# RMS norm on one core: ScalarE squares without summing, GpSimd scales part of the rows, VectorE code is aligned, the last tile is loaded whole

## The chip, the cores and the metric

The kernel runs on one core of one Trainium2 chip. The metric is device time in microseconds (us), the median of several executions. The *span* of a profile is a little shorter than that time: 160.0 against 161.79 us in the profiled execution of the kernel before. All runs told here are with a granted clock of 1.00.

In the profile's lines, DVE is VectorE, ACT is ScalarE, POOL is GpSimd, SP is SyncE (it issues all large transfers here), PE is TensorE, and DMA stands for the core's sixteen transfer engines. SBUF is the on-chip memory that holds the tiles; PSUM is a second one, which takes the squares and, after the change, gamma. "L95" is line 95 of the kernel whose profile is shown; an edit can shift the numbers by a few lines.

## The reference

```python
x: (16, 1024, 512) float32;  gamma: (512,) float32, all ones
rms = np.sqrt(np.mean(x ** 2, axis=-1, keepdims=True) + 1e-5)
return (x / rms * gamma).astype(np.float32)
```

There are 16,384 rows of 512 elements: 33.55 MB to read and as much to write.

## The kernel before

The rows make four tiles; a tile is 128 partitions of 32 rows each (8 MB). The kernel keeps three tiles in SBUF at once, so tile 3 goes into the slot of tile 0 and can be loaded only when tile 0 has been stored (its load is issued at 81.86 us, after a wait of 8.6 us for that store). SyncE issues everything in one fixed order:

```python
groups = [(t, g) for t in range(4) for g in range(0, R, G)]     # R = 32, G = 8 rows
slot_of = [0, 1, 2, 0]
def transfers(t, g):                 # after the group at row g of tile t has been scaled
    if (t, g) == (0, 0):
        store(0, 0, 0, 1);  load(1, 1, 0, 32);  load(2, 2, 0, 16)
        store(0, 0, 1, 2);  load(2, 2, 16, 32)
    elif (t, g) == (0, 24):  store(0, 0, 2, 32)
    elif (t, g) == (1, 8):
        store(1, 1, 0, 16)
        load(3, 0, 0, 16)            # tile 3 in two halves
        load(3, 0, 16, 32)
    elif (t, g) == (1, 24):  store(1, 1, 16, 32)
    elif (t, g) == (2, 24):  store(2, 2, 0, 32)
    elif (t, g) == (3, 8):   store(3, 0, 0, 16)
    elif (t, g) == (3, 24):  store(3, 0, 16, 32)
```

Half of the groups are squared and summed by ScalarE alone, row by row; for the other half ScalarE squares four rows at a time into PSUM and VectorE sums them. VectorE scales every row:

```python
if (g // G) % 2:
    for h in range(0, G, H):                                     # H = 4
        sq = psum.tile([P, H, D], fp32, name="sq")
        nc.scalar.activation(out=sq, in_=slots[slot][:, g+h : g+h+H, :], func=AF.Square)
        nc.vector.tensor_reduce(out=ss[:, h : h+H], in_=sq, axis=..., op=OP.add)
else:
    for r in range(G):
        nc.scalar.activation(out=sq_scratch, in_=slots[slot][:, g+r, :],
                             func=AF.Square, accum_out=ss[:, r : r+1])
... sqrt on ScalarE, reciprocal on VectorE ...
for r in range(G):
    nc.vector.scalar_tensor_tensor(out=row, in0=row, scalar=rstd[:, r : r+1],
                                   in1=gamma_b, op0=OP.mult, op1=OP.mult)   # gamma_b in SBUF
```

Of the kernel before, what the change touches and what calls it, by code (L numbers as in the profile page):

```python
# [1 line left out]

# [4 lines left out]


@with_exitstack
def kernel(  # L10
    ctx: ExitStack,
    tc: tile.TileContext,
    x: bass.AP,
    gamma: bass.AP,
    out: bass.AP,
):
    nc = tc.nc
    P = nc.NUM_PARTITIONS
    eps = 1e-5
    fp32 = mybir.dt.float32  # L20
    AF = mybir.ActivationFunctionType
    OP = mybir.AluOpType

    xf = x.flatten_outer_dims()
    of = out.flatten_outer_dims()
    N, D = xf.shape
    R = 32
    G = 8
    H = 4
    assert N == 4 * P * R  # L30

    xv = xf.rearrange("(t p r) d -> t p r d", p=P, r=R)
    ov = of.rearrange("(t p r) d -> t p r d", p=P, r=R)

    const = ctx.enter_context(tc.tile_pool(name="const", bufs=1))
    stats = ctx.enter_context(tc.tile_pool(name="stats", bufs=4))
    psum = ctx.enter_context(tc.tile_pool(name="psum", bufs=2, space=bass.MemoryType.PSUM))

    slots = [const.tile([P, R, D], fp32, name=f"slot{i}") for i in range(3)]

    def load(t, slot, r0, r1):
        nc.sync.dma_start(out=slots[slot][:, r0:r1], in_=xv[t][:, r0:r1])  # L42

    def store(t, slot, r0, r1):
        nc.sync.dma_start(out=ov[t][:, r0:r1], in_=slots[slot][:, r0:r1])

    load(0, 0, 0, 8)
    load(0, 0, 8, 32)

    gamma_row = const.tile([1, D], fp32)  # L50
    nc.scalar.dma_start(out=gamma_row, in_=gamma.unsqueeze(0))
    ones_col = const.tile([1, P], fp32)
    nc.vector.memset(ones_col, 1.0)  # L53
    gamma_psum = psum.tile([P, H, D], fp32, name="sq")
    nc.tensor.matmul(gamma_psum[:, 0], ones_col, gamma_row, start=True, stop=True)  # L55
    gamma_b = const.tile([P, D], fp32)
    nc.vector.tensor_copy(out=gamma_b, in_=gamma_psum[:, 0])  # L57

    eps_t = const.tile([P, 1], fp32)
    nc.vector.memset(eps_t, eps)  # L60
    sq_scratch = const.tile([P, D], fp32)

    def row_stats(slot, g):
        ss = stats.tile([P, G], fp32, name="ss")
        rms = stats.tile([P, G], fp32, name="rms")
        rstd = stats.tile([P, G], fp32, name="rstd")
        if (g // G) % 2:
            for h in range(0, G, H):
                sq = psum.tile([P, H, D], fp32, name="sq")
                nc.scalar.activation(out=sq, in_=slots[slot][:, g + h : g + h + H, :], func=AF.Square)  # L70
                nc.vector.tensor_reduce(  # L71
                    out=ss[:, h : h + H], in_=sq, axis=mybir.AxisListType.X, op=OP.add
                )
        else:
            for r in range(G):
                nc.scalar.activation(  # L76
                    out=sq_scratch,
                    in_=slots[slot][:, g + r, :],
                    func=AF.Square,
                    accum_out=ss[:, r : r + 1],  # L80
                )
        nc.scalar.activation(out=rms, in_=ss, func=AF.Sqrt, bias=eps_t, scale=1.0 / D)  # L82
        nc.vector.reciprocal(out=rstd, in_=rms)  # L83
        return rstd

    def apply(slot, g, rstd):
        for r in range(G):
            nc.vector.scalar_tensor_tensor(  # L88
                out=slots[slot][:, g + r, :],
                in0=slots[slot][:, g + r, :],  # L90
                scalar=rstd[:, r : r + 1],
                in1=gamma_b,
                op0=OP.mult,
                op1=OP.mult,
            )  # L95

    groups = [(t, g) for t in range(4) for g in range(0, R, G)]
    slot_of = [0, 1, 2, 0]

    def transfers(t, g):  # L100
        if (t, g) == (0, 0):
            store(0, 0, 0, 1)
            load(1, 1, 0, 32)
            load(2, 2, 0, 16)
            store(0, 0, 1, 2)
            load(2, 2, 16, 32)
        elif (t, g) == (0, 24):
            store(0, 0, 2, 32)
        elif (t, g) == (1, 8):
            store(1, 1, 0, 16)  # L110
            load(3, 0, 0, 16)
            load(3, 0, 16, 32)
        elif (t, g) == (1, 24):
            store(1, 1, 16, 32)
        elif (t, g) == (2, 24):
            store(2, 2, 0, 32)
        elif (t, g) == (3, 8):
            store(3, 0, 0, 16)
        elif (t, g) == (3, 24):
            store(3, 0, 16, 32)  # L120

    ahead = row_stats(0, 0)
    for k, (t, g) in enumerate(groups):
        rstd = ahead
        if k + 1 < len(groups):
            tn, gn = groups[k + 1]
            ahead = row_stats(slot_of[tn], gn)
        apply(slot_of[t], g, rstd)
        transfers(t, g)


# [1 line left out]
_INS = ['x', 'gamma']  # L133
_OUTS = [((16, 1024, 512), 'float32')]


# [23 lines left out]
```

## Time and profile before

| | before |
|---|---|
| time, median | 162.27 us (3 runs), 162.15 us in the rounds with the change |
| transfer queue, share of sixteen engines' span | 97.9% |
| VectorE busy | 122.6 us (77%) |
| ScalarE busy | 80.1 us (50%) |
| GpSimd busy | 0.2 us |
| last store issued | 146.62 us |

The page of the kernel before: the span in 40 slices (each digit is the busy share of a slice in tenths; the DMA row is the mean of the sixteen transfer engines), and the queue that carries all of x.

```profile
span 160.0 us, 409 instructions
...
DVE  0101928999999509999999999999999999996000
...
DMA  5999999699699999997999999999996996999993
...
q1 hardware_dynamic: 2160, 67.11, 97.9%
```

The costliest groups of instructions of the page (line, engine, operation, output and inputs, shape, count; busy time and mean ns of one; idle time just before them and what ended it).

```profile
L88 DVE SCALAR_TENSOR_TENSOR slot<-slot,rstd,gamma_b 128x512 f32<-128x512 f32 x128 | 85.8, 741 | 0.1
L76 ACT ACTIVATE sq_scratch<-slot 128x512 f32<-128x512 f32 x64 | 40.0, 625 | 10.0 <-DMA slot<-in_x_dram 8.7
L70 ACT ACTIVATE sq<-slot 128x2048 f32<-128x2048 f32 x16 | 29.8, 1865 | 18.8 <-DVE ss L71 11.5
L71 DVE TENSOR_REDUCE ss<-sq 128x4 f32<-128x2048 f32 x16 | 35.9, 2277 | 3.6 <-ACT sq L70 3.6
```

The transfers bound this kernel. From the records of single packets, no gap shows in any of the sixteen engines between the first load and the last store; the dips of the digits are the edges of packets of up to 2.6 us. Compute matters only where a store is issued too late to keep the queue full. The timeline of VectorE and SyncE at the end (start, length in us, what) shows how near that is: the last store goes out at 146.62 us, right after VectorE's last row.

```profile
136.62 9.97 DVE L88 SCALAR_TENSOR_TENSOR slot<-slot,rstd,gamma_b 128x512 f32<-128x512 f32 x15
146.62 0.33 SPq L45 DMA_DIRECT2D out_dram<-slot  x1
```

### The profile page before, as it was taken

Reading aid. Unit: us, or ns where it says so; the run is one execution under the profiler, and the core shown is the slowest. Engines: PE = TensorE matmul, PEld = TensorE weight load, DVE = VectorE, ACT = ScalarE, POOL = GpSimd, SP = SyncE. Lnnn points to the kernel's source line nnn. Section 1 sums busy time; section 2 is a strip of 40 time slices with the busy share of each in tenths; the row PEclk is TensorE's granted clock in tenths of the full one; section 3 lists DMA queues with packets and bytes.
Section 4 is the critical chain, followed back from the end, with each engine's and each line's share of the span. In section 5 each row is a group of like instructions: output and inputs, shape, how many; then the busy total and the mean of one; then the engine's idle time right before and its main releaser. Section 6 shows DMA issues by size and latency. Waiting matters only on the chain.

```text
span 160.0 us, 409 instructions
## 1 busy us (share of the span) xinstructions
PE 2.0 (1%) x2; PEld 0.5 (0%) x2; DVE 122.6 (77%) x163; ACT 80.1 (50%) x162; POOL 0.2 (0%) x4
## 2 busy tenths in 40 slices
PE   4000000000000000000000000000000000000000
PEld 1000000000000000000000000000000000000000
DVE  0101928999999509999999999999999999996000
ACT  3098029991291999996900960069709950000000
POOL 0000000000000000000000000000000000000000
DMA  5999999699699999997999999999996996999993
GB/s 197 524 393 393 430 487 508 279 524 491 295 395 396 456 467 434 494 461 323 445 393 475 426 410 426 475 410 410 491 524 295 508 491 295 467 434 410 426 475 147
DMA packets 2164, 67.13 MB, mean 420 GB/s; under 512 B 241, under 2 KB 241, under 8 KB 498
## 3 DMA queue, kind: packets, MB, share of 16 engines
q1 hardware_dynamic: 2160, 67.11, 97.9%
q14 instruction: 2, 0.02, 0.0%
q10 hardware_dynamic: 2, 0.00, 0.0%
HBM read 33.56 MB, written 33.55 MB: 419 GB/s over the span
## 4 chain that ended last, share of the span: by engine, by line
DVE 67%; DMA 14%; ACT 7%; issue 2%; DVEq 0%; SPq 0%
DVE slot L88 48%; DVE ss L71 18%; DMA slot<-in_x_dram 14%; ACT sq_scratch L76 3%; ACT sq L70 3%; DVE rstd L83 1%; ACT rms L82 1%; DVEq L155 0%; SPq L42 0%
## 5 line engine op out<-in xcount | busy, mean ns | idle before, releaser
L88 DVE SCALAR_TENSOR_TENSOR slot<-slot,rstd,gamma_b 128x512 f32<-128x512 f32 x128 | 85.8, 741 | 0.1
L76 ACT ACTIVATE sq_scratch<-slot 128x512 f32<-128x512 f32 x64 | 40.0, 625 | 10.0 <-DMA slot<-in_x_dram 8.7
L70 ACT ACTIVATE sq<-slot 128x2048 f32<-128x2048 f32 x16 | 29.8, 1865 | 18.8 <-DVE ss L71 11.5
L71 DVE TENSOR_REDUCE ss<-sq 128x4 f32<-128x2048 f32 x16 | 35.9, 2277 | 3.6 <-ACT sq L70 3.6
L82 ACT ACTIVATE rms<-ss,eps_t 128x8 f32<-128x8 f32 x16 | 4.6, 297 | 26.2 <-DVE ss L71 26.0
L83 DVE RECIPROCAL rstd<-rms 128x8 f32<-128x8 f32 x16 | 3.1, 196 | 16.3 <-ACT rms L82 16.3
L76 ACT ACTIVATION_READ_ACCUMULATOR sq_scratch<-slot 128x1 f32 x64 | 11.9, 186 | 0.0
L57 DVE COPY gamma_b<-sq 128x512 f32<-128x512 f32 x1 | 0.7, 691 | 3.3 <-PE sq L55 3.3
L55 PE MATMUL sq<-gamma_row,ones_col 1*128 1x512 f32 x2 | 2.0, 1122 | 2.2 <-DMA gamma_row<-in_gamma_dram 2.2
L76 ACT ACT_TABLE_LOAD x1 | 1.3, 1283 | 1.3 <-PEq L144 1.3
L82 ACT ACT_TABLE_LOAD x1 | 1.3, 1283 | 0.0
L53 DVE MEMSET ones_col<- 1x128 f32 x1 | 0.2, 165 | 0.8 <-PEq L144 0.8
L55 PEld LDWEIGHTS sq<-gamma_row,ones_col 1*128 1x128 f32 x2 | 0.5, 308 | 2.1 <-issue 2.1
L144 POOL MEMSET const-uint8-127<- 128x1 uint8 x1 | 0.1, 102 | 0.0
L144 POOL MEMSET const-bfloat16-1.0<- 128x1 bf16 x1 | 0.1, 101 | 0.0
L144 POOL MEMSET const-float32-0.0<- 128x1 f32 x1 | 0.1, 98 | 0.2 <-issue 0.2
L144 POOL MEMSET const-float32-1.0<- 128x1 f32 x1 | 0.1, 98 | 0.0
L60 DVE MEMSET eps_t<- 128x1 f32 x1 | 0.1, 59 | 0.0
## 6 DMA issues: line engine op xcount, KB each, us to landing
slot<-in_x_dram SPq DMA_DIRECT2D x4, 4096.0 KB, 32.1
out_dram<-slot SPq DMA_DIRECT2D x4, 4096.0 KB, 18.4
out_dram<-slot SPq DMA_DIRECT2D x1, 7680.0 KB
slot<-in_x_dram SPq DMA_DIRECT2D x1, 6144.0 KB, 21.6
slot<-in_x_dram SPq DMA_DIRECT2D x1, 2048.0 KB, 7.2
out_dram<-slot SPq DMA_DIRECT2D x2, 256.0 KB, 21.4
gamma_row<-in_gamma_dram ACTq DMA_DIRECT2D x1, 2.0 KB
slot<-in_x_dram SPq DMA_DIRECT2D x1, 25.9
```

Source lines behind the costliest of these rows:

```text
L53: nc.vector.memset(ones_col, 1.0)
L55: nc.tensor.matmul(gamma_psum[:, 0], ones_col, gamma_row, start=True, stop=True)
L57: nc.vector.tensor_copy(out=gamma_b, in_=gamma_psum[:, 0])
L60: nc.vector.memset(eps_t, eps)
L70: nc.scalar.activation(out=sq, in_=slots[slot][:, g + h : g + h + H, :], func=AF.Square)
L71: nc.vector.tensor_reduce(out=ss[:, h : h + H], in_=sq, axis=mybir.AxisListType.X, op=OP.add)
L76: nc.scalar.activation(out=sq_scratch, in_=slots[slot][:, g + r, :], func=AF.Square, accum_out=ss[:, r : r + 1],)
L82: nc.scalar.activation(out=rms, in_=ss, func=AF.Sqrt, bias=eps_t, scale=1.0 / D)
L83: nc.vector.reciprocal(out=rstd, in_=rms)
L88: nc.vector.scalar_tensor_tensor(out=slots[slot][:, g + r, :], in0=slots[slot][:, g + r, :], scalar=rstd[:, r : r + 1], in1=gamma_b, op0=O ...
L144: nc = _bacc.Bacc("TRN2", target_bir_lowering=False, num_devices=1)
```

## The change

The intent is to shorten ScalarE's work and VectorE's scaling. ScalarE squares and no longer sums, up to seven rows in one instruction, alternately into PSUM and SBUF; VectorE sums all rows; GpSimd scales three of 8, five of 12 or six of 16 rows of a group in two passes (by 1/rms, then by gamma); VectorE reads gamma from PSUM; VectorE's code is aligned in memory by one line, `addr_align(128)`; tile 3 is loaded by one transfer; the groups grow from 8 rows to 12 and 16. The core of the diff:

```diff
+    nc.vector.addr_align(128, offset=0, max_nops=0)
...
-    nc.scalar.dma_start(out=gamma_row, in_=gamma.unsqueeze(0))
+    for c in (slice(0, D // 2), slice(D // 2, D)):
+        nc.scalar.dma_start(out=gamma_row[:, c], in_=gamma.unsqueeze(0)[:, c])
...
+    first = [(0, 8, (4, 4), 3), (8, 12, (7, 5), 5), (20, 12, (7, 5), 5)]
+    later = [(0, 16, (7, 5, 4), 6), (16, 16, (7, 5, 4), 6)]   # row, rows, pieces, GpSimd's share
...
+        for k, m in enumerate(pieces):
+            sq = (SBUF tile of 5 rows) if k % 2 else (PSUM tile of 7 rows)
+            nc.scalar.activation(out=sq[:, :m], in_=rows, func=AF.Square)
+            nc.vector.tensor_reduce(out=ss[:, r : r + m], in_=sq[:, :m], axis=..., op=OP.add)
...
+        for r in range(n - share):
             nc.vector.scalar_tensor_tensor(
-                in1=gamma_b,
+                in1=gamma_psum,
...
+        part = x[:, n - share :, :]
+        by_row = rstd[:, n - share : n].to_broadcast([P, share, D])
+        nc.gpsimd.tensor_tensor(out=part, in0=part, in1=by_row, op=OP.mult)
+        nc.gpsimd.tensor_tensor(out=part, in0=part, in1=gamma_b.to_broadcast([P, share, D]), op=OP.mult)
...
-            load(3, 0, 0, 16)
-            load(3, 0, 16, 32)
+            load(3, 0, 0, 32)
```

## The prediction

The forecast's sum is 162.1 us, against 162.15 us measured before: it took the parts of the change to be worth next to nothing. Terms that came from no trace or run are cut where a cut is marked: in the GpSimd item the time of one instruction and of two passes ("half of that" means half of that time; the 6.6 us that stands is ten VectorE rows at 0.66 us), in the walk the lateness at that speed, in the last item what the alignment would remove. The walk's 1.6 and 2.0 ns an element are speeds that I assumed, as the kernel before has no GpSimd arithmetic.

> **What bounds the kernel now.** The data transfers. The page gives the load and store queue 97.9% of sixteen engines' span of 160.0 us, with 67.11 MB moved. The packet records show all sixteen engines busy with no gap from about 1.2 us (the first load, in the chain of waits) to about 158 us; the rest is the start and the last landing. VectorE is busy 122.6 us (77%), ScalarE 80.1 us (50%), and neither sets the time as long as each store is issued before the queue runs dry. That margin is small: VectorE finishes its last row and the last store is issued at 146.6 us (timeline), and I place the end of the store ahead of it at about 147.5 us. The second tile-sized store (tile 2) is issued at about 115.9 us for a queue that runs dry near 118.5 us.
>
> **What the change does.**
> - ScalarE: 64 single-row squares with accumulator reads (625 + 186 ns each) go; the 16 four-row ones (1865 ns) become 22 of four to seven rows, about 3.1 us for seven (estimate from 1865 ns per four rows and 625 ns per one). ScalarE falls from 80 to about 60 us. Worth nothing: it is not on the limiting path.
> - VectorE: all 128 rows are now summed there, about 0.56 us a row (2277 ns per four): 36 becomes about 71 us. 49 of 128 row scalings leave (at about 0.66 us pitch, 741 ns each): 86 becomes about 53 us. The sum stays near 123 us.
> - GpSimd: 49 rows, each passed over twice. No GpSimd arithmetic is in this trace. [...] The six-to-ten split suggests that its author saw about half of that: ten VectorE rows take 6.6 us.
> - gamma read from PSUM leaves VectorE one SBUF tensor input, which should spare it waits for GpSimd [...].
> - The whole last load moves the same bytes in larger packets: under 0.1 us, and its first half lands about 9 us later (near 109 us), which VectorE, busy with tile 2 until then, hardly notices.
> - Code placement [...] off the limiting path.
>
> **How much is on the critical path.** Nearly none. I walked the new instruction order against the store deadlines. With GpSimd at or under 1.6 ns an element every store is in time, tightest the first half of tile 3 (issued near 137, needed near 138 us); VectorE ends near 144 us. At 2.0 the last store is late by about 2.5 us[...].
>
> **Prediction.** 162.1 us, 80% range 161.5 to 163.8. Faster by over 2%: 0.02; within 2%: 0.86; slower by over 2%: 0.12.
>
> **What would show it.** Right: queue share still about 97 to 98%, no dip of the transfer rate in the 40 slices, VectorE's busy time near 123 us, ScalarE's near 60, six-row GpSimd passes at or under 5 us each, last store issued before 147 us. Wrong: transfer slices near zero around 137 us or 147 to 152 us, and a chain of waits that runs through GpSimd into the last store.
>
> **What would make it wrong.** GpSimd passes of 6.5 us or more; VectorE slowed by GpSimd, or by the PSUM operand (0.1 us a row is 8 us in all, and the margins are 1 to 3 us); slower transfers while GpSimd works. A gain beyond 1% would need transfers faster than the 433 GB/s that whole packets already show.

Two of its terms have since been shown. With gamma in PSUM, VectorE is spared waits for GpSimd: beside GpSimd's passes a scaling takes 741 ns in the mean, and 1626 ns with gamma in SBUF (e4, below). And "under 0.1 us" agrees with the trace of the kernel before: 32 KB packets take 1.213 us and 64 KB packets 2.418 us (medians; sixteen of the latter at once are the 433 GB/s), which saves 8 ns on each of a tile's eight large packets per engine, 0.06 us.

## The result

| | before | after |
|---|---|---|
| time, median of 6 runs | 162.15 us | 167.31 us |
| ratio | | 1.0317, 95% interval 1.0303 to 1.0331 |
| queue share | 97.9% | 95.0% |
| VectorE / ScalarE / GpSimd busy | 122.6 / 80.1 / 0.2 us | 124.3 / 63.5 / 98.6 us |
| last store issued | 146.62 us | 153.33 us |

Every ratio in this document is the mean time of one kernel's fast runs over that of the other's of the same rounds, so it is not quite the ratio of the medians quoted. The change is 3.2% slower, above the predicted range.

The page of the changed kernel: slices, queue and the groups that answer to those above.

```profile
span 165.2 us, 273 instructions
...
DVE  0037803989999999999999999993899999980000
...
DMA  5999979969998999998899799989969983885885
...
q1 hardware_dynamic: 2016, 67.11, 95.0%
...
L105 POOL TENSOR_TENSOR slot<-slot,rstd 128x3072 f32<-128x3072 f32 (+2 forms) x9 | 43.5, 4834 | 53.4 <-DVE rstd L89 53.4
L79 DVE TENSOR_REDUCE ss<-sq_psum 128x7 f32<-128x3584 f32 (+1 forms) x15 | 47.0, 3132 | 21.2 <-ACT sq_psum L78 21.2
...
L106 POOL TENSOR_TENSOR slot<-slot,gamma_b 128x3072 f32<-128x3072 f32 (+2 forms) x9 | 54.7, 6081 | 0.7
L95 DVE SCALAR_TENSOR_TENSOR slot<-slot,rstd,gamma_psum 128x512 f32<-128x512 f32 x79 | 53.1, 741 | 0.2
```

VectorE's sum of work is nearly as it was (1.7 us more), and a scaling costs the same 741 ns with gamma in PSUM. The DMA digits fall to 3 and 5 near the end. The next view, busy time of the engines in stretches of 4 us near the end (the last two columns are the DMA share and GB/s; a share above 1 is an effect of packets counted whole), shows two holes, at 138 to 142 and at 150 to 154 us. The kernel before has none in these stretches (second fence).

```profile
134.00:138.00 4.00, 0.00 (x0) 0.00 (x0) 4.00 (x5) 1.05 (x2) 4.00 (x1) 1.00 0.91 393
138.00:142.00 4.00, 0.00 (x0) 0.00 (x0) 3.96 (x8) 0.00 (x0) 3.14 (x2) 1.00 0.25 107
142.00:146.00 4.00, 0.00 (x0) 0.00 (x0) 4.00 (x7) 0.00 (x0) 4.00 (x1) 1.00 1.02 434
146.00:150.00 4.00, 0.00 (x0) 0.00 (x0) 1.89 (x3) 0.00 (x0) 3.92 (x2) 1.00 0.91 393
150.00:154.00 4.00, 0.00 (x0) 0.00 (x0) 0.00 (x0) 0.00 (x0) 3.30 (x1) 1.00 0.31 131
```

```profile
138.00:142.00 4.00, 0.00 (x0) 0.00 (x0) 4.00 (x7) 0.00 (x0) 0.00 (x0) 1.00 0.91 393
150.00:154.00 4.00, 0.00 (x0) 0.00 (x0) 0.00 (x0) 0.00 (x0) 0.00 (x0) 1.00 0.95 410
```

In the packet records the sixteen engines stand idle for 2.9 us on average ahead of the store of tile 3's first half and for 2.5 us ahead of its second: 5.4 us, against 5.2 us between the two spans (165.2 less 160.0). So two stores were late, and the question is what made them late. The timeline of the changed kernel at the turn from tile 2 to tile 3 and at the end:

```profile
106.33 6.67 DVE L95 SCALAR_TENSOR_TENSOR slot<-slot,rstd,gamma_psum 128x512 f32<-128x512 f32 x10
112.99 3.16 ACT L78 ACTIVATE sq_psum<-slot 128x3584 f32<-128x3584 f32 x1 [13.10 <-DMA slot<-in_x_dram]
116.19 3.89 DVE L79 TENSOR_REDUCE ss<-sq_psum 128x7 f32<-128x3584 f32 x1 [3.19 <-ACT sq_psum L78]
...
136.99 4.03 DVE L95 SCALAR_TENSOR_TENSOR slot<-slot,rstd,gamma_psum 128x512 f32<-128x512 f32 x6
141.09 12.57 SPq L45 DMA_DIRECT2D out_dram<-slot  x2
141.26 5.31 POOL L105 TENSOR_TENSOR slot<-slot,rstd 128x3072 f32<-128x3072 f32 x1 [0.86 <-DVE rstd L89]
146.65 6.66 POOL L106 TENSOR_TENSOR slot<-slot,gamma_b 128x3072 f32<-128x3072 f32 x1
```

ScalarE waits 13.1 us for the whole load and starts at 112.99 us. VectorE is done with tile 2 at 113.0 us, but must still wait 3.19 us, because a square of seven rows (3.16 us) has to come first. The first-half store goes out at 141.09 us, after VectorE's last row of that half. The last store goes out at 153.33 us (the second of the two issues, which end at 141.09 + 12.57), right after GpSimd's two passes of 5.31 and 6.66 us.

### The profile page after: what moved, and what is told of

The parts are those of the page before. It is cut to its first block, busy times and chain, and to the rows that moved or that the text cites. A ratio compares the mean times of both kernels' runs of the same rounds, so it can differ in the third digit from the quotient of the medians.

```text
span 165.2 us, 273 instructions
## 1 busy us (share of the span) xinstructions
PE 2.0 (1%) x2; PEld 0.5 (0%) x2; DVE 124.3 (75%) x112; ACT 63.5 (38%) x36; POOL 98.6 (60%) x24
## 4 chain that ended last, share of the span: by engine, by line
DMA 47%; DVE 16%; POOL 15%; ACT 7%; POOLq 4%; issue 3%; SPq 0%; DVEq 0%; ACTq 0%
DMA slot<-in_x_dram 32%; DMA out_dram<-slot 15%; DVE ss L79 12%; POOL slot L105 9%; POOL slot L106 7%; ACT sq_psum L78 6%; POOLq L163 4%; DVE slot L95 4%; ACT sq_sbuf L78 1%; DVE rstd L89 0%; SPq L42 0%; DVEq L95 0%; ACTq L78 0%; POOLq L105 0%
## 5 line engine op out<-in xcount | busy, mean ns | idle before, releaser
L105 POOL TENSOR_TENSOR slot<-slot,rstd 128x3072 f32<-128x3072 f32 (+2 forms) x9 | 43.5, 4834 | 53.4 <-DVE rstd L89 53.4
L79 DVE TENSOR_REDUCE ss<-sq_psum 128x7 f32<-128x3584 f32 (+1 forms) x15 | 47.0, 3132 | 21.2 <-ACT sq_psum L78 21.2
L78 ACT ACTIVATE sq_psum<-slot 128x3584 f32<-128x3584 f32 (+1 forms) x15 | 38.4, 2559 | 49.2 <-DVE ss L79 26.4
L106 POOL TENSOR_TENSOR slot<-slot,gamma_b 128x3072 f32<-128x3072 f32 (+2 forms) x9 | 54.7, 6081 | 0.7
L95 DVE SCALAR_TENSOR_TENSOR slot<-slot,rstd,gamma_psum 128x512 f32<-128x512 f32 x79 | 53.1, 741 | 0.2
L79 DVE TENSOR_REDUCE ss<-sq_sbuf 128x5 f32<-128x2560 f32 (+1 forms) x9 | 24.7, 2745 | 0.5 <-ACT sq_sbuf L78 0.5
L78 ACT ACTIVATE sq_sbuf<-slot 128x2560 f32<-128x2560 f32 (+1 forms) x9 | 20.5, 2279 | 2.6 <-DVE ss L79 2.6
L88 ACT ACTIVATE rms<-ss,eps_t 128x16 f32<-128x16 f32 (+2 forms) x9 | 2.7, 299 | 12.1 <-DVE ss L79 12.1
L89 DVE RECIPROCAL rstd<-rms 128x16 f32<-128x16 f32 (+2 forms) x9 | 2.1, 234 | 1.7 <-ACT rms L88 1.7
L56 PE MATMUL gamma_psum<-gamma_row,ones_col 1*128 1x512 f32 x2 | 2.0, 1118 | 6.5 <-DMA gamma_row<-in_gamma_dram 6.5
```

The costliest lines, as they stand in the source:

```text
L56: nc.tensor.matmul(gamma_psum, ones_col, gamma_row, start=True, stop=True)
L78: nc.scalar.activation(out=sq[:, :m], in_=rows, func=AF.Square)
L79: nc.vector.tensor_reduce(out=ss[:, r : r + m], in_=sq[:, :m], axis=mybir.AxisListType.X, op=OP.add)
L88: nc.scalar.activation(out=rms[:, :n], in_=ss[:, :n], func=AF.Sqrt, bias=eps_t, scale=1.0 / D)
L89: nc.vector.reciprocal(out=rstd[:, :n, 0], in_=rms[:, :n])
L95: nc.vector.scalar_tensor_tensor(out=x[:, r, :], in0=x[:, r, :], scalar=rstd[:, r], in1=gamma_psum, op0=OP.mult, op1=OP.mult,)
```

## The experiments

Theory A, formed from these lines: the first late store is set by the late landing of the whole load and VectorE's work after it, the second by GpSimd's twelve microseconds. Rival C is my prediction's own worry: GpSimd alone. Rival B: GpSimd's work slows the transfers.

### Each suspected cause alone, and both (e1, e2, e3)

e1 undoes the whole load:

```diff
-            load(3, 0, 0, 32)
+            load(3, 0, 0, 16)
+            load(3, 0, 16, 32)
```

> The changed kernel with the last tile loaded in two halves again (the scheduler then also puts one reciprocal ahead of a 5-row sum). Theory A (two late stores: the last tile's start is set by the landing of the whole load, its end by 12.0 us of GpSimd passes): VectorE no longer waits 3.2 us at 113 us, the first reciprocal of tile 3 comes near 122.4 us instead of 128.0, the first-half store is in time (near 138 us), the last store is issued near 150 us instead of 153.3; about 164.1 us. Rival C (GpSimd alone, the load does not matter): 167.3 us as the changed kernel. Rival B (GpSimd slows the transfers themselves): 167 us, one-row-of-transfer times above those of before.

e2 removes GpSimd's second pass; the result is right only because gamma is all ones:

```diff
-        nc.gpsimd.tensor_tensor(out=part, in0=part, in1=gamma_b.to_broadcast([P, share, D]), op=OP.mult)
```

> The changed kernel without GpSimd's second pass (the multiplication by gamma; right here only because gamma is all ones), the load still whole. Theory A: the last store is no longer late, as VectorE ends near 148 us; but the first-half store of tile 3 is still issued at 141 us, 2.6 us late, set by VectorE after the late landing; about 164.9 us. Rival C: all of the loss goes, 162.2 us. Rival B: about half of the loss goes in proportion to GpSimd's busy time (98.6 to about 44 us), 164.5 us, but with slower transfers and no gap before the first-half store.

e3 has both edits.

> Both: load in halves and no second GpSimd pass. Theory A: both stores of tile 3 in time (issued near 138 and 145 us), no gap in the transfers, 162.2 us, same as before. Rival C: 162.2 us too. Rival B: 164 to 165 us, as GpSimd is still busy for 44 us.

| run | time | ratio to before | mean idle ahead of first-half / last store |
|---|---|---|---|
| changed kernel | 167.31 us | 1.0317 | 2.9 / 2.5 us |
| e1, load in halves | 164.10 us | 1.0146 | 0.0 / 2.3 us |
| e2, one GpSimd pass | 164.24 us | 1.0152 | 2.8 / 0.0 us |
| e3, both | 163.94 us | 1.0121 | 0.0 / 0.0 us |

In e1 and e2 each edit closes one hole and leaves the other, as theory A said. The same stretches, first e1 (its hole now lies in 146 to 150 us), then e2:

```profile
138.00:142.00 4.00, 0.00 (x0) 0.00 (x0) 4.00 (x7) 0.00 (x0) 4.00 (x1) 1.00 0.92 393
146.00:150.00 4.00, 0.00 (x0) 0.00 (x0) 0.00 (x0) 0.00 (x0) 4.00 (x1) 1.00 0.55 238
```

```profile
138.00:142.00 4.00, 0.00 (x0) 0.00 (x0) 3.96 (x8) 0.00 (x0) 0.93 (x1) 1.00 0.34 147
150.00:154.00 4.00, 0.00 (x0) 0.00 (x0) 0.00 (x0) 0.00 (x0) 0.00 (x0) 1.00 1.10 475
```

C falls: e1 leaves GpSimd alone and still takes off 1.7 points, and e2 stays 1.5% slower than before. B cannot be dropped by the times, as it forecast 164.5 us for e2 and 164 to 165 us for e3, close to what came out. The packets speak against it: the 64 KB packets after the first 25 us take 2.42 us (median) in the changed kernel and in the kernel before. And e8 below, with GpSimd busy for 94.8 us, takes the time of the kernel before. In e1 the wait of 3.19 us is gone (VectorE goes straight from tile 2 to a sum at 112.79 us). But e3 is a miss: both holes are closed, and it is still 1.2% slower than before instead of equal. Something else held 2 us. (Its four runs spread from 162.89 to 164.20 us, more than those of the other runs here, so this remainder is known to about a third only: the ratio's 95% interval is 1.0086 to 1.0156.)

The windows of e3 at the end show it. Below, e3 first, then the kernel before:

```profile
156.00:158.00 2.00, 0.00 (x0) 0.00 (x0) 0.00 (x0) 0.00 (x0) 0.00 (x0) 1.00 0.84 360
158.00:160.00 2.00, 0.00 (x0) 0.00 (x0) 0.00 (x0) 0.00 (x0) 0.00 (x0) 1.00 0.08 33
```

```profile
156.00:158.00 2.00, 0.00 (x0) 0.00 (x0) 0.00 (x0) 0.00 (x0) 0.00 (x0) 1.00 0.68 295
158.00:160.00 2.00, 0.00 (x0) 0.00 (x0) 0.00 (x0) 0.00 (x0) 0.00 (x0) 1.00 0.00 0
```

A DMA share of 0.08 is about one engine of sixteen. In the packet records of e3, chained by the packet that begins where another ends, fifteen engines finish within 0.45 us of one another and one 2.3 us after the last of them. That kernel, like the changed one, has an 8 KB instruction fetch 3.8 us into the span, in the middle of the first load; the kernel before has its fetches at 47 and 65 us. (The expectation of e5 below says 2.4, 3.4, 46 and 64; the packet records, on the timelines' zero, give the figures here.) This led to theory D: the alignment of VectorE's code moves a fetch into the first load and makes one transfer engine late.

### The alignment (e5, e6, e10)

e5 is e3 without the alignment, e10 the changed kernel without it, and e6 the kernel before with it and nothing else:

```diff
-    nc.vector.addr_align(128, offset=0, max_nops=0)     # e5 and e10; e6 adds this line to before
```

> Run e3 came out at 163.94 us though both stores of tile 3 were issued in time (137.6 and 144.9 us) and the queue had no gap; the packet records show one of the sixteen transfer engines finishing 2.4 us after the others. That engine carried an 8 KB instruction fetch 3.4 us into the first load, which before does not have there (its two fetches come at 46 and 64 us). This is e3 without the alignment of VectorE's code. Theory D (the alignment causes that early fetch, and the fetch makes one transfer engine late): no 8 KB fetch during the first load, no late engine at the end, 162.0 us. Rival E (the rest of the loss comes from elsewhere, e.g. GpSimd's remaining 44 us or gamma fetched in two pieces): 163.9 us and the late engine as in e3.

> The kernel before with the alignment of VectorE's code alone added. Theory D: an 8 KB fetch during the first load, one transfer engine 1 to 2.5 us late at the end, 163 to 164 us. Rival E: 161.8 us as before.

> The changed kernel without the alignment of VectorE's code, nothing else. Theory D: no 8 KB fetch in the first load, no transfer engine late, so the whole last load lands about 1.5 us earlier (near 111.4 us instead of 113.0, as in e7), VectorE waits less, the last store is issued 1.5 to 2 us earlier than 153.3: about 165.6 us. If the late engine is hidden in the changed kernel by the gaps in its queue: 167.3 us.

| run | time | ratio to before | 8 KB fetch in the first load | ScalarE starts on the second load | tile 3's load issued |
|---|---|---|---|---|---|
| before | 162.27 us | | no | 22.82 us | 81.86 us |
| e6, before + alignment | 164.80 us | 1.0152 | yes | 24.12 us | 83.73 us |
| changed kernel | 167.31 us | 1.0317 | yes | 24.16 us | 83.70 us |
| e10, without alignment | 165.54 us | 1.0209 | no | 22.86 us | 81.73 us |
| e3 | 163.94 us | 1.0121 | yes | 23.93 us | 83.92 us |
| e5, without alignment | 162.23 us | 1.0002 | no | 22.76 us | 81.74 us |

All three came out as theory D said, though e6 lost more than its 163 to 164 us: its late engine ends 3.1 us after the others. One line costs 1.5% on the kernel before and 1.1 to 1.2 points of ratio in the changed ones. The path can be read in the ordinary views: with the line, the second load is usable 1.3 us later, tile 0's store has landed and frees its slot 1.9 to 2.2 us later, and tile 3's whole load lands at 112.99 instead of 111.21 us (in e10). The timelines of ScalarE, first before, then e6, then e10, show the first of these:

```profile
22.82 3.68 ACT L70 ACTIVATE sq<-slot 128x2048 f32<-128x2048 f32 x2 [7.30 <-DMA slot<-in_x_dram]
```

```profile
24.12 3.68 ACT L72 ACTIVATE sq<-slot 128x2048 f32<-128x2048 f32 x2 [7.64 <-DMA slot<-in_x_dram]
```

```profile
22.86 3.16 ACT L76 ACTIVATE sq_psum<-slot 128x3584 f32<-128x3584 f32 x1 [5.60 <-DMA slot<-in_x_dram]
```

The second load became usable only when its slowest engine was done: in the packet records of the changed kernel fifteen engines end it by 22.54 us and one at 23.82 us, and ScalarE starts on it at 24.16 us. In the kernel before all sixteen end it by 22.50 us, and ScalarE starts at 22.82 us.

Theory D is shown as far as the alignment goes: adding the line brings the early fetch (one packet of 8 KB that takes 0.31 us; on the kernel before, the line also makes three fetches of the two at 47 and 65 us, e6), the late landings and the loss, taking it away removes all three. That the fetch itself is the cause rests on the packet records, as no run moved a fetch by other means. They show that the late engine is the one with the fetch. In the changed kernel the fetch ends at 4.15 us; the x packet that follows it without a gap takes 1.14 us where the others of its size take 0.61 us (median), and that engine starts its next packets at 8.35 us, the other fifteen theirs at 7.18 to 7.56 us. The slow packet stands right after the early fetch in all six runs with the alignment, and none of the seven without it has a late engine there. A fetch elsewhere slows its follower too (at 47 us in the kernel before, 1.49 us instead of 1.21 us), with no loss of time that shows. Why the lag then grows from 0.8 us to 1.3 us by the end of the second load, and further later on, was not settled.

### The whole load on the kernel before (e7)

```diff
-            load(3, 0, 0, 16)
-            load(3, 0, 16, 32)
+            load(3, 0, 0, 32)
```

> The kernel before with the last tile loaded whole, nothing else. Theory A: tile 3's squares can start only near 113 us instead of 108 us or earlier, VectorE has about 3 us to wait, ends near 149.5 us instead of 146.6, and the last store is 2 to 3 us late: 164 to 165 us. Rival (only the changed kernel, with its slower sums and GpSimd, suffers from the whole load): 161.8 us.

It took 165.51 us, a ratio of 1.0205. The rival falls: this one edit costs 3.3 us on a kernel with no GpSimd work at all. VectorE, which before goes on with the next reciprocal at 120.21 us (first fence), now waits 5.39 us and goes on at 125.59 us (second):

```profile
115.81 4.48 DVE L71 TENSOR_REDUCE ss<-sq 128x4 f32<-128x2048 f32 x2
120.21 0.19 DVE L83 RECIPROCAL rstd<-rms 128x8 f32<-128x8 f32 x1
```

```profile
115.71 4.49 DVE L71 TENSOR_REDUCE ss<-sq 128x4 f32<-128x2048 f32 x2
125.59 0.20 DVE L83 RECIPROCAL rstd<-rms 128x8 f32<-128x8 f32 x1 [5.39 <-ACT rms L82]
```

### What is left of GpSimd (e11, e8, e12)

e11 is the changed kernel with the load in halves and without the alignment. e8 is e11 with one more edit, four rows for GpSimd in the very last group:

```diff
+    groups[-1] = (3, 16, 16, (7, 5, 4), 4)
```

e12 is e11 with three rows of sixteen for GpSimd from tile 1 on:

```diff
-    later = [(0, 16, (7, 5, 4), 6), (16, 16, (7, 5, 4), 6)]
+    later = [(0, 16, (7, 5, 4), 3), (16, 16, (7, 5, 4), 3)]
```

> The changed kernel with the last load in halves and without the alignment, both GpSimd passes and six rows in every group. What is left of the loss is GpSimd's last two passes: VectorE's last reciprocal near 136.7 us (as in e8), passes 12.0 us, last store issued near 149.1 us where the queue runs dry near 147.7: about 163.4 us.

> A mended form of the change: last load in halves, GpSimd takes four rows instead of six in the last group only, no alignment; all else as changed, both GpSimd passes kept. Theory A with D: GpSimd ends the last group near 146 us (four rows: 3.6 + 4.5 us from 137.7), VectorE near 145.6; last store issued at about 146 us, in time; 162 us, the same as before. If GpSimd or its second pass costs something beyond the two late stores: above 163 us.

> As e11, but GpSimd takes three rows of sixteen everywhere from tile 1 on, so its passes take about 6.2 us a group. Theory F: VectorE, which now sums all rows, cannot take the rows back: five groups ahead of the last grow by 2.0 us each (three rows of 0.66 us), the last reciprocal comes near 146.6 us, the last store near 155.4: about 170 us. Rival (GpSimd's slow passes are the whole trouble and a smaller share mends it): 162.2 us.

e11 took 162.66 us (ratio 1.0028), better than the 163.4 expected: its last store is issued at 148.88 us, and the transfer engines idle 1.2 us ahead of it. e8 took 162.20 us (1.0004): last store at 145.28 us, no hole. So GpSimd's six rows of the last group cost about 0.5 us once the other two causes are gone. As e8 still has the sums on VectorE, the larger groups, the two-piece fetch of gamma and most of GpSimd's work, none of these costs time that shows. e12 took 169.99 us (1.0477). VectorE cannot take the rows back, because it now sums all 128 rows: its last reciprocal moves from 136.50 us in e11 (first fence) to 146.28 us (second).

```profile
136.50 0.24 DVE L87 RECIPROCAL rstd<-rms 128x16 f32<-128x16 f32 x1
136.77 6.67 DVE L93 SCALAR_TENSOR_TENSOR slot<-slot,rstd,gamma_psum 128x512 f32<-128x512 f32 x10
```

```profile
146.28 0.24 DVE L87 RECIPROCAL rstd<-rms 128x16 f32<-128x16 f32 x1
146.56 8.65 DVE L93 SCALAR_TENSOR_TENSOR slot<-slot,rstd,gamma_psum 128x512 f32<-128x512 f32 x13
```

No version beat the kernel before: e5 and e8 reach its time, since with no hole in the queue the transfers set the time.

### Gamma in SBUF instead of PSUM (e4)

```diff
-                in1=gamma_psum,
+                in1=gamma_b[:, 0],
```

> The changed kernel with VectorE reading gamma from SBUF instead of PSUM (the scheduler moves a few sums as well). If two SBUF inputs of VectorE and GpSimd's reads shut each other out, scalings that meet a GpSimd pass wait for up to 5 to 7 us or GpSimd's passes stretch: mean scaling over 1 us or six-row passes over 7 us, and 172 us or more. If they do not disturb each other: 741 ns, 5.3 and 6.7 us as now, and 167 us.

It took 222.01 us (ratio 1.3724). The groups by shape, the changed kernel first, then e4:

```profile
L95 DVE SCALAR_TENSOR_TENSOR slot<-slot,rstd,gamma_psum 128x512 f32<-128x512 f32 x79 | 53.1, 741 | 0.2
L106 POOL TENSOR_TENSOR slot<-slot,gamma_b 128x3072 f32<-128x3072 f32 x6 | 40.1, 6681 | 0.5
L105 POOL TENSOR_TENSOR slot<-slot,rstd 128x3072 f32<-128x3072 f32 x6 | 31.8, 5308 | 22.1 <-DVE rstd L89 22.1
```

```profile
L95 DVE SCALAR_TENSOR_TENSOR slot<-slot,rstd,gamma_b 128x512 f32<-128x512 f32 x79 | 123.4, 1626 | 0.2
L106 POOL TENSOR_TENSOR slot<-slot,gamma_b 128x3072 f32<-128x3072 f32 x6 | 41.2, 6870 | 0.5
L105 POOL TENSOR_TENSOR slot<-slot,rstd 128x3072 f32<-128x3072 f32 x6 | 31.9, 5310 | 66.0 <-DVE rstd L89 66.0
```

And from the timeline of e4, one scaling that met one pass:

```profile
78.57 5.90 DVE L95 SCALAR_TENSOR_TENSOR slot<-slot,rstd,gamma_b 128x512 f32<-128x512 f32 x1
78.61 5.31 POOL L105 TENSOR_TENSOR slot<-slot,rstd 128x3072 f32<-128x3072 f32 x1 [15.85 <-DVE rstd L89]
```

The single scaling lasts 5.90 us: it ends at 84.47 us, 0.55 us after the pass (83.92 us). GpSimd's passes barely stretch (5.31 us as before and 6.87 instead of 6.68 us); VectorE pays (1626 instead of 741 ns a scaling in the mean). What makes VectorE wait, and what decides which of the two waits, the runs do not show: the scaling starts 0.04 us ahead of the pass and yet outlasts it. So one part of the change was sound and needed: without gamma in PSUM, the change would have cost 60 us rather than 5.

## Why the prediction was wrong

- **What bounds the kernel: right.** The queue's share and its unbroken run set the time, and compute counts only through the issue times of the last stores. e5 and e8, which keep the queue full with quite different compute, land within 0.05% of before.
- **The busy times: right.** Predicted near 123 us for VectorE and 60 us for ScalarE; measured 124.3 and 63.5 us (there are 24 squares of several rows, not 22). The PSUM operand cost nothing (741 ns both ways).
- **GpSimd's speed: wrong, the first failed step.** I put two passes over six rows near the 6.6 us of ten VectorE rows, because "the six-to-ten split suggests that its author saw about half of that": an estimate of mine, with no GpSimd arithmetic in the trace to check it. The trace of the changed kernel has 5.31 us for a pass of 3,072 elements by one value per row and 6.68 us for one by gamma repeated over rows, 1.73 and 2.17 ns an element (each time over 3,072). An author's tuning is not a measurement. What it costs depends on what else is undone: taking out the second pass alone, which is more than a faster GpSimd would save, takes off 1.65 points (e2), but with the other two causes gone all of GpSimd's lateness is worth 0.3% (e11).
- **The whole load: wrong, the second failed step.** "VectorE, busy with tile 2 until then, hardly notices" was wrong twice. The load was usable at 112.99 us, not near 109 (111.21 us without the alignment, e10). And I compared its landing with the moment VectorE becomes free, although ScalarE's square of 3.16 us stands between the two. The walk had tile 3's first half issued near 137 us; it was issued at 141.09 us, and at 136.65 us in e11, with the load in halves and no alignment. Undoing it is worth 1.7 points of the 3.2 (e1), or 1.8 if the alignment has gone first (e10 to e11); on the kernel before it costs 2.05% (e7).
- **The alignment: wrong, the third failed step.** I expected it to act "off the limiting path". It brought a fetch into the first load (it ends at 4.15 us), on the limiting path, the transfer engines themselves. Nor did it remove the pause of 0.66 us in VectorE's chain at 139.30 us of the kernel before: one of that length is still there with the line (e6, 140.62 us; e3, 138.57 us), and no fetch packet lies near it in the kernel before, where they come at 47 and 65 us. The cost: 1.1 points (changed kernel to e10), 1.2 (e3 to e5), 1.5 on the kernel before (e6).
- **The sum.** From the changed kernel's 3.17% excess, taking away alignment and whole load leaves 0.28% (e11), and two rows fewer in the last group 0.04% (e8). The parts overlap, so undone one by one from the changed kernel they add up to more than the whole (1.7, 1.65 and 1.1 points). The two passes together run at 1.95 ns an element (11.97 us for 6,144), for which the walk of store deadlines has, at 2.0, "late by about 2.5 us"; with the other causes gone the hole is 1.2 us (e11). Among the signs named as "wrong", the low slices and the chain through GpSimd into the last store did appear; had I stopped at them, I would have blamed GpSimd alone. One undone part at a time showed otherwise.

## What to carry to other kernels

In a kernel bound by its transfers, walk the deadline of every late store, and count what must run between a landing and the work that you think is waiting: here the single larger transfer saved nothing that shows and put off the first use by 9.9 us (101.34 us in e11, 111.21 us in e10). Instruction fetches ran on the same transfer engines as the data (the fetch that ends at 4.15 us has an x packet right behind it), so a change of code placement belongs in the transfer trace and in a run of its own. Before handing VectorE's work to GpSimd, look whether VectorE's other input can come from PSUM (beside GpSimd's passes a scaling took 741 ns with gamma there and 1626 ns with it in SBUF, e4), and take GpSimd's speed from a measurement.
